# Splitting the 32x32 products of a triangular inverse over several steps, and copying accumulator banks out earlier, in a one-core decoder trunk

## The chip, the cores and the metric

The kernel runs on one core of a Trainium2 chip. The metric is the device time of one execution in microseconds (us), as the median of several runs.

The engines are named as the profile names them. PE is the matrix engine (PEld its weight loads), DVE the vector engine, ACT the scalar engine with its tables of functions, POOL the third elementwise engine, and SP the engine that here only issues DMAs. PSUM is the accumulator memory into which PE writes: eight banks, each of 128 partitions x 512 f32. SBUF is the on-chip memory for everything else.

## The reference, cut to what matters

One layer of a decoder trunk over 512 tokens of width 2048. The hidden state `h` goes through one wide projection, whose columns feed two token mixers. The change is almost wholly in the second, the chunked gated delta rule (GDN): per head and chunk it solves a unit lower triangular system, and its output is gated by `silu(z)`.

```python
p = h @ w_in[l]
c_q, c_kv, k_pe, q_g, k_g, v_g, z, b_logit, a_logit, gate_logits = _split_cols(p)
y_a = _mla_branch(c_q, c_kv, ...) @ w_o_mla[l]
y_b = _gdn_branch(qkv, z, ...) @ w_o_gdn[l]
...
# inside the GDN branch
Lmat = jnp.where(strict, jnp.einsum('bhncd,bhnsd->bhncs', kb, k) * decay, 0.0)
A = Lmat + jnp.eye(CHUNK, dtype=jnp.float32)
sol = lax.linalg.triangular_solve(A, rhs, left_side=True, lower=True, unit_diagonal=True)
...
o = o * lax.rsqrt(jnp.mean(o * o, axis=-1, keepdims=True) + EPS) * gdn_norm
o = o * jax.nn.silu(z)
...
# the channel mixer
gate, up = jnp.split(h @ w_gate_up[l], 2, axis=-1)
x = x + gt_f * ((jax.nn.silu(gate) * up) @ w_down[l])
```

## The kernel before, in words

**Products.** Every large product keeps about f32 accuracy by splitting each operand into a rounded high part and a remainder (`hi`, `lo`), and issuing three matmuls (hi x hi, hi x lo, lo x hi). Weights come in by DMA (`raw`), ACT casts `hi` (L270, or L1888 in the Strassen products), DVE subtracts to get `lo` (L271, L1895). A "set" of units accumulates over k in four PSUM banks and hands them to a `done` function.

**Order.** PE, POOL and SP instructions keep the order in which the program is written; ACT and DVE instructions are placed by the compiler's scheduler around them, which also assigns PSUM banks and SBUF slots. The order of PE is made by `Driver`. It runs the units of the big products one after the other; whenever 12 matmuls have been counted (`GROUP`), it calls `pump`, which gives each of the side chains (Python generators in the list `drv.chains`, in the order in which they were added) one step. `yield n` in a chain means that it sits out n steps. `hold` at the end of a set takes 12 off the count, so that the first step after it comes a group later. A chain's matmuls therefore stand between matmuls of the big product, in one lump per step.

**The GDN chain** (`gdn(g)`, once for heads 0 to 3 and once for heads 4 to 7). It makes `LT`, solves the 32x32 diagonal blocks on DVE (`fsX`, L801 to L808), writes the result to DRAM by two POOL DMAs (`fso`, L810) and reads it back by four POOL DMAs into the four 32-partition strips of `T32` (L814). Fourteen steps later 32 matmuls of 32x32 form `M1` in one PSUM bank (L823 to L830), ACT copies it out (L832, L833); six steps later 64 matmuls of 32x32 form `X1` in another bank (L835 to L844), from which ACT and DVE write into `T64` and `T64T`. The profile leaves numbers out of names, so `M1` stands there as `M`, `X1` as `X`, and `T32` as `T` (as does `T64`). An f32 matmul is counted as two instructions in the profile, so a lump of 32 shows as x64.

The first group's chain runs beside the sets `k47` and `v47` (profile names `k` and `v`), the second group's beside `cq`, `ckv` and `z1` (`cq`, `ckv`, `z`). Next to it in the second case run the chains that transpose the normed `cq` and `ckv` (`cT`, L986 to L993, one bank for each of four k, read by ACT at L249 and DVE at L250) and the rope chain, which puts two transposed tiles into two banks (`kpT`, L1046 to L1050).

**The z sets.** When set `z0` or `z1` ends, `z_done` applies silu to the four banks, straight from PSUM, on ACT (L946). The banks are free for the next sets only after that. After `z0` comes the set `cq`.

**The last transposed bank.** In the channel mixer, gate products are transposed in PSUM (`turned_a`, name `aT`). For blocks s < 8 a bank is copied to SBUF (`f`, L2165); for the others it is split straight from PSUM, by an ACT cast and a DVE subtraction (`hilo`, L244 and L247). The last such bank is s = 10, b = 3. After it begins the first Strassen down product, whose four products take all eight banks.

Of the kernel before, what the change touches and what calls it, by code (L numbers as in the profile page):

```python
# [11 lines left out]
AF = mybir.ActivationFunctionType  # L12
# [5 lines left out]
NT = 4  # L18
# [155 lines left out]
def block_kernel(ctx: ExitStack, tc: tile.TileContext, a: dict, out):  # L174
    nc = Core(tc, PINNED)
# [12 lines left out]
    def nm(s):  # L188
        serial[0] += 1
        return f"{s}_{serial[0]}"  # L190

    def S(s, dt=F32):
        return slots.tile([P, 512], dt, tag="s", name=nm(s))

    def PS(s):
        return psum.tile([P, 512], F32, tag="ps", name=nm(s))
# [7 lines left out]
    def side(dst, src):  # L204
        nc.gpsimd.dma_start(dst, src)

    def behind(ins):
        return tc.keep_in_program_order(ins)
# [3 lines left out]
    def tok(j):  # L212
        return slice(j * P, (j + 1) * P)
# [26 lines left out]
    def hilo(src, name, scale=None, late=False):  # L240
        hi, lo = S(name + "h", F32R), S(name + "l", F32R)
        n = src.shape[1]
        if scale is None:
            cast = nc.scalar.copy(hi[:, 0:n], src)  # L244
            if late:
                behind(cast)
            nc.vector.tensor_tensor(lo[:, 0:n], src, hi[:, 0:n].bitcast(F32), ALU.subtract)  # L247
        else:
            nc.scalar.activation(hi[:], src, AF.Copy, scale=scale)  # L249
            nc.vector.scalar_tensor_tensor(lo[:], src, scale, hi[:].bitcast(F32), op0=ALU.mult, op1=ALU.subtract)  # L250
        return hi, lo
# [454 lines left out]
    def gdn(g):  # L706
# [82 lines left out]
        for hf in range(2):  # L789
            s = S("fsL")  # L790
# [22 lines left out]
        for b in range(4):  # L813
            side(T32[32 * b:32 * b + 32, :].rearrange("p (n a) -> p n a", a=32),  # L814
                                fso[g][b].rearrange("c h i a -> i (c h) a"))
        yield 14
        T64 = [S("T64"), S("T64")]
        T64T = [S("T64T"), S("T64T")]
        for w in T64 + T64T:
# [2 lines left out]
        nc.vector.transpose(T32T[:], T32[:])  # L822
        p1 = PS("M1")  # L823
        for c in range(NT):
            for i in range(4):
                n0 = 128 * c + 32 * i
                for pa in (0, 64):
                    pb = pa + 32
                    mm(p1[pb:pb + 32, n0:n0 + 32], LT[c][pa:pa + 32, 128 * i + pb:128 * i + pb + 32],
                       T32[pa:pa + 32, n0:n0 + 32], start=True, stop=True, tile_position=(pa, pb))  # L830
        M1 = S("M1")
        nc.scalar.copy(M1[32:64, :], p1[32:64, :])  # L832
        nc.scalar.copy(M1[96:128, :], p1[96:128, :])  # L833
        yield 6
        p2 = PS("X1")  # L835
        for c in range(NT):
            for i in range(4):
                n0 = 128 * c + 32 * i
                s = slice(n0, n0 + 32)
                for pa in (0, 64):  # L840
                    pb = pa + 32
                    A_, B_ = slice(pa, pa + 32), slice(pb, pb + 32)
                    mm(p2[B_, s], T32T[B_, s], M1[B_, s], start=True, stop=True, tile_position=(pb, pb))
                    mm(p2[A_, s], M1[B_, s], T32T[B_, s], start=True, stop=True, tile_position=(pb, pa))  # L844
        v32 = lambda ap: ap.rearrange("p (n a) -> p n a", a=32)
        v64 = lambda ap: ap.rearrange("p (n a) -> p n a", a=64)
        for hf in range(2):
# [29 lines left out]
        for hf in range(2):  # L877
# [6 lines left out]
            for c in (2 * hf, 2 * hf + 1):  # L884
                nc.vector.tensor_scalar(h4(TT[c][:])[0:64, :, 64:128], v64(p4[0:64, 256 * (c % 2):256 * (c % 2) + 256]),
                                        -1.0, None, op0=ALU.mult)
        del T64, T64T, T32, T32T, M1, M2, LT
        yield
# [52 lines left out]
    def z_done(g, chain):  # L941
        def done(ps):
            sz = []
            for t in range(NT):
                s = S("sz")
                nc.scalar.activation(s[:], ps[t][:], AF.Silu)  # L946
                sz.append(s)

            def gen():
                while chain() in drv.chains:  # L950
                    yield
                for t in range(NT):
                    o = S("oz")
                    nc.scalar.dma_start(o[:], o_dram[t, g])
                    yield
                    for i in range(4):
                        nc.vector.scalar_tensor_tensor(sz[t][:, tok(i)], o[:, tok(i)], fo[:, t, 4 * g + i:4 * g + i + 1],
                                                       sz[t][:, tok(i)], op0=ALU.mult, op1=ALU.mult)
                    nc.scalar.dma_start(u_dram[t, g], sz[t][:])
                    yield  # L960
            drv.add(gen())
        return done
# [697 lines left out]
    def mixing():  # L1660
# [25 lines left out]
        def start_a():  # L1686
            ch["A"] = drv.add(gdn(0))
# [6 lines left out]
        def start_b():  # L1694
            ch["B"] = drv.add(gdn(1))
# [444 lines left out]
    def turned_a(b):  # L2140

        box = {}

        def one(n):
            if not turning:
                return
            s, tiles = turning[0]
            if s == 0:
                if b < 2:
                    gu_turn(1, b, tiles, n, box)  # L2150
                elif (b, n) == (3, 3):
                    turning.pop(0)
                return
            x, t = divmod(n, 2)
            if n == 0:
                box["ps"] = PS("aT")
            if s < 8:
                h, f = b % 2, 2 * (b // 2) + x
            else:
                h, f = x, b  # L2160
            nc.tensor.transpose(box["ps"][:, tok(n)], tiles[h, t][:, tok(f)], ident)
            if n == 3:
                if s < 8:
                    f_ = S("f")
                    nc.scalar.copy(f_[:], box["ps"][:])  # L2165
                    side(f_dram[2 * s + b // 2, h], f_[:])
                    stored.add((2 * s + b // 2, h))
                else:
                    kept_a(4 * s + b, hilo(box["ps"][:], "a"))
                if b == 3:  # L2170
                    turning.pop(0)

        return [lambda n=n: one(n) for n in range(4)]

    def kept_a(k, hl):

        if 36 <= k < 40:
            aT[k] = hl
        else:
            for i in range(2):  # L2180
                side(a_dram[k - 32, i], hl[i][:].bitcast(F32))
# [95 lines left out]
    def gu_turn(s, h, f, n, box):  # L2277

        x, t = divmod(n, 2)
        if n == 0:  # L2280
            box["ps"] = PS("guT")
        nc.tensor.transpose(box["ps"][:, tok(n)], f[h][:, 256 * t + 128 * x:256 * t + 128 * x + 128], ident)
        if n == 3:
            f_ = S("f")
            nc.scalar.copy(f_[:], box.pop("ps")[:])
            del f[h]
            side(f_dram[s, h], f_[:])
            stored.add((s, h))
# [334 lines left out]
```

## Time and profile before

| | |
|---|---|
| time, median of 3 runs | 2711.08 us (2708.78 to 2713.11) |
| the profiled execution | 2706.44 us, of which 2704.6 us from first to last instruction (the span) |
| granted PE clock | 0.999 of full |
| PE busy | 2683.6 us, 99% of the span, 13046 matmuls |
| PEld busy | 2237.3 us, 83% |
| DVE busy | 2087.6 us, 77% |
| ACT busy | 1201.6 us, 44% |
| POOL busy | 228.6 us, 8% |

In a line of the timeline, the first number is the start in us from the start of the span, the second the time taken, then the engine, the line of the kernel, the operation and "output <- inputs"; in brackets stands how long the engine sat idle before, and what ended that. All PE instructions pass through a helper and carry L157, so tile names tell them apart. A 128x512 matmul lasts about 0.39 us, but matmuls overlap: one starts every 0.227 us.

### The profile page before, as it was taken

The numbers are of one execution on the slowest core, as the hardware profiler recorded it, in microseconds if no ns is written. First come the engines' busy times: TensorE is split into PE (matmuls) and PEld (weight loads), VectorE is DVE, ScalarE is ACT, GpSimd is POOL, SyncE is SP. The second block draws the span as 40 slices with busy tenths as digits, with TensorE's granted clock in tenths as the row PEclk, the third lists the DMA queues.
The fourth block names the chain that finished last, engine by engine and source line by source line (L and its number), as shares of the span: only waits on it lengthen the run. The fifth ranks groups of instructions, "written<-read, shape, count | busy, mean of one in ns | idle before, by whom it ended". The sixth has DMA issues, their size and how long they took to land.

```text
span 2704.6 us, 36528 instructions
## 1 busy us (share of the span) xinstructions
PE 2683.6 (99%) x13046; PEld 2237.3 (83%) x13046; DVE 2087.6 (77%) x3230; ACT 1201.6 (44%) x1720; POOL 228.6 (8%) x310
## 2 busy tenths in 40 slices
PE   9999999999999999999999999999999999999998
PEld 7888788888888888888888888888888888888886
DVE  8785666777768866768788778788878888788786
ACT  3443432453245333234574444444444446545454
POOL 0000002011100000000010000001101101011012
PEclk9999999999999999999999999999999999999999
DMA  9897565646664867854763566567767777788595
GB/s 372 306 351 268 158 192 177 201 152 191 187 172 136 286 223 285 306 187 134 272 193 120 193 209 208 202 218 250 243 227 263 252 249 212 210 238 226 179 278 154
DMA packets 312126, 600.45 MB, mean 222 GB/s; under 512 B 42852, under 2 KB 69636, under 8 KB 311816
## 3 DMA queue, kind: packets, MB, share of 16 engines
q1 hardware_dynamic: 257160, 486.52, 54.7%
q0 software_dynamic: 21888, 59.83, 8.3%
q10 hardware_dynamic: 32896, 51.78, 5.2%
q8 instruction: 102, 1.67, 0.3%
q14 instruction: 80, 0.66, 0.1%
HBM read 507.80 MB, written 90.20 MB: 221 GB/s over the span
## 4 chain that ended last, share of the span: by engine, by line
PE 98%; DVE 1%; ACT 1%; issue 0%; DMA 0%; SPq 0%; DVEq 0%; ACTq 0%
PE m L157 43%; PE gb L157 6%; PE v L157 4%; PE z L157 3%; PE ya L157 3%; PE ga L157 3%; PE k L157 3%; PE s L157 3%; PE q L157 3%; PE yb L157 3%; PE wo L157 3%; PE gu L157 3%; PE dn L157 2%; PE qk L157 2%; PE dnt L157 2%; PE ckv L157 2%
## 5 line engine op out<-in xcount | busy, mean ns | idle before, releaser
L1888 ACT CAST hi<-raws 128x1024 fp32r<-128x1024 f32 (+1 forms) x360 | 322.9, 907 | 575.3 <-DVE raws L1868 346.9
L1895 DVE TENSOR_TENSOR lo<-raws,hi 128x1024 fp32r<-128x1024 f32 (+1 forms) x360 | 376.0, 1046 | 176.5 <-ACT hi L1888 168.9
L270 ACT CAST hi<-raw 128x1024 fp32r<-128x1024 f32 x262 | 271.9, 1041 | 489.8 <-DMA raw<-in_w_in_dram 130.7
L271 DVE TENSOR_TENSOR lo<-raw,hi 128x1024 fp32r<-128x1024 f32 x262 | 320.7, 1227 | 190.2 <-ACT hi L270 183.6
L442 DVE CUSTOM_DVE_ANT_0 rawm<-rawm,cbc 128x1024 f32<-128x1024 f32 x192 | 233.9, 1234 | 3.8 <-DMA rawm<-in_w_mod_dram 3.5
L157 PE MATMUL m<-hi,h2h 128*128 128x512 f32 x480 | 190.7, 397 | 0.0
L157 PE MATMUL m<-hi,h2l 128*128 128x512 f32 x480 | 187.4, 390 | 0.0
L157 PE MATMUL m<-lo,h2h 128*128 128x512 f32 x480 | 186.9, 389 | 0.0
L157 PE MATMUL m<-hi,xh 128*128 128x512 f32 x448 | 174.6, 390 | 0.7 <-DVE al L247 0.7
L157 PE MATMUL m<-hi,xl 128*128 128x512 f32 x448 | 174.4, 389 | 0.0
L157 PE MATMUL m<-lo,xh 128*128 128x512 f32 x448 | 174.4, 389 | 0.0
L1895 DVE TENSOR_TENSOR lo<-sums,hi 128x1024 fp32r<-128x1024 f32 x120 | 146.7, 1222 | 22.2 <-ACT hi L1888 22.1
L1868 DVE TENSOR_TENSOR sums<-raws,raws 128x1024 f32<-128x1024 f32 x120 | 146.2, 1219 | 3.6 <-DMA raws<-in_w_down_dram 3.6
L1888 ACT CAST hi<-sums 128x1024 fp32r<-128x1024 f32 x120 | 126.1, 1051 | 36.1 <-PE m L157 22.5
L157 PEld LDWEIGHTS m<-hi,h2l 128*128 128x128 f32 x480 | 90.1, 188 | 19.4
L157 PEld LDWEIGHTS m<-lo,h2h 128*128 128x128 f32 x480 | 90.4, 188 | 17.8
L157 PEld LDWEIGHTS m<-hi,h2h 128*128 128x128 f32 x480 | 90.2, 188 | 17.3
L157 PE MATMUL gb<-hh,hi 128*128 128x512 f32 x256 | 102.4, 400 | 0.0
L157 PE MATMUL gb<-hh,lo 128*128 128x512 f32 x256 | 100.0, 391 | 0.0
L157 PE MATMUL gb<-hl,hi 128*128 128x512 f32 x256 | 99.9, 390 | 0.0
L157 PEld LDWEIGHTS m<-hi,xh 128*128 128x128 f32 x448 | 84.1, 188 | 18.8 <-DVE al L247 1.1
L157 PEld LDWEIGHTS m<-hi,xl 128*128 128x128 f32 x448 | 84.1, 188 | 17.6
(587 smaller groups left out, 6844.5 us busy)
## 6 DMA issues: line engine op xcount, KB each, us to landing
raws<-in_w_gate_up_dram SPq DMA_DIRECT2D x400, 256.0 KB, 4.0
rawm<-in_w_mod_dram SPq DMA_DIRECT2D x192, 512.0 KB, 5.5
raw<-in_w_in_dram SPq DMA_DIRECT2D x144, 512.0 KB, 5.0
raws<-in_w_down_dram SPq DMA_DIRECT2D x160, 256.0 KB, 5.2
s_dram<-raws ACTq DMA_DIRECT2D x88, 256.0 KB, 3.5
raws<-s_dram SPq DMA_DIRECT2D x88, 256.0 KB, 4.3
rawa<-in_w_in_dram SPq DMA_DIRECT2D x32, 512.0 KB, 5.6
raw<-in_w_o_dram SPq DMA_DIRECT2D x24, 512.0 KB, 6.9
```

The source lines that it names most:

```text
L157: return self.tc.keep_in_program_order(f(*args, **kwargs))
L270: nc.scalar.copy(hi[:], raw[:])
L271: (lo_eng or nc.vector).tensor_tensor(lo[:], raw[:], hi[:].bitcast(F32), ALU.subtract)
L442: r = nc.vector.tensor_tensor_reduce(raw, raw, c, 1.0, 0.0, ALU.mult, ALU.add, parts[:, k, half:half + 1])
L1868: add = lambda o, x, y: behind(nc.vector.tensor_tensor(o, x, y, ALU.add))
L1888: nc.scalar.copy(hi[:], src)
L1895: nc.vector.tensor_tensor(lo[:], src, hi[:].bitcast(F32), ALU.subtract)
```

## The change

Three edits, in `gdn`, `z_done` and `turned_a`.

1. The four banks of `z0` are copied to SBUF, t = 0 and 2 by DVE and t = 1 and 3 by ACT. Silu is applied to the SBUF tiles in the first step of the z chain, which yields once more for that. `z1` is as it was.
2. The copy of the bank s = 10, b = 3 to SBUF is an ACT copy of its own, and the cast and the subtraction read that SBUF tile.
3. The `M1` products start two steps earlier and come in two parts in consecutive steps; the `X1` products come in four parts in four consecutive steps, the first 4 steps after the last `M1` part, where they were one lump 6 steps after. The last part of `X1` comes in the same step as the whole lump did before, and what follows keeps its steps.

```diff
@@ gdn
-        yield 14
+        yield 12
         T64 = [S("T64"), S("T64")]
...
                     mm(p1[pb:pb + 32, n0:n0 + 32], LT[c][pa:pa + 32, 128 * i + pb:128 * i + pb + 32],
                        T32[pa:pa + 32, n0:n0 + 32], start=True, stop=True, tile_position=(pa, pb))
+            if c == 1:
+                yield
         M1 = S("M1")
         nc.scalar.copy(M1[32:64, :], p1[32:64, :])
         nc.scalar.copy(M1[96:128, :], p1[96:128, :])
-        yield 6
+        yield 4
         p2 = PS("X1")
         for c in range(NT):
...
                     mm(p2[B_, s], T32T[B_, s], M1[B_, s], start=True, stop=True, tile_position=(pb, pb))
                     mm(p2[A_, s], M1[B_, s], T32T[B_, s], start=True, stop=True, tile_position=(pb, pa))
+            if c < NT - 1:
+                yield
@@ z_done
                 s = S("sz")
-                nc.scalar.activation(s[:], ps[t][:], AF.Silu)
+                if g:
+                    nc.scalar.activation(s[:], ps[t][:], AF.Silu)
+                else:
+                    (nc.scalar.copy if t % 2 else nc.vector.tensor_copy)(s[:], ps[t][:])
                 sz.append(s)
...
                 while chain() in drv.chains:
                     yield
+                if not g:
+                    for t in range(NT):
+                        nc.scalar.activation(sz[t][:], sz[t][:], AF.Silu)
+                    yield
                 for t in range(NT):
@@ turned_a
-                    kept_a(4 * s + b, hilo(box["ps"][:], "a"))
+                    src = box["ps"]
+                    if s == 10 and b == 3:
+                        src = S("f")
+                        nc.scalar.copy(src[:], box["ps"][:])
+                    kept_a(4 * s + b, hilo(src[:], "a"))
```

## The prediction

> **What bounds the kernel now.** I read the page first: the busy shares, then the chain that ended last. From them the question is only what PE does and waits for.
>
> ```profile
> PE 2683.6 (99%) x13046; PEld 2237.3 (83%) x13046; DVE 2087.6 (77%) x3230; ACT 1201.6 (44%) x1720; POOL 228.6 (8%) x310
> ...
> PE 98%; DVE 1%; ACT 1%; issue 0%; DMA 0%; SPq 0%; DVEq 0%; ACTq 0%
> ```
>
> PE is busy 2683.6 of 2704.6 us, so 21 us is all that waits could give back; the rest is matmuls, and the change removes none of those. Next I read whom PE waited for, in the list of waits of PE:
>
> ```profile
> PE cb L157 <- DMA crow<-in_c_dram: 3.0, 1, 3.0
> PE cT L157 <- DVE cql L250: 1.6, 1, 1.6
> ...
> PE cq L157 <- ACT sz L946: 0.9, 1, 0.9
> ...
> PE m L157 <- DVE al L247: 0.7, 1, 0.7
> ...
> PE cq L157 <- ACT E L766: 0.3, 1, 0.3
> ```
>
> Four of these rows lie where the change works: `cq` behind the silu of `z0`, `m` behind the last transposed bank, `cT` in the step that also holds the `X` lump, and `cq` behind `E`. They sum to 3.5 us. A measurement of this kernel can tell about 0.2%, or 5.4 us, from no change. So these waits cannot make a measurable gain even if all go; the question is what the new order of PE costs. I price each edit in PE time, because whatever PE loses is the kernel's time.
>
> **Edit 1, the z0 banks.** From the timeline around the end of `z0`:
>
> ```profile
> 636.85 0.40 PE L157 MATMUL cq<-hi,hl 128*128 128x512 f32 x1
> ...
> 636.94 0.60 ACT L766 ACTIVATE E<-pE 128x512 f32<-128x512 f32 x1
> 637.55 1.28 ACT L946 ACT_TABLE_LOAD   x1
> ...
> 637.59 0.50 PE L157 MATMUL cq<-hi,hh 128*128 128x512 f32 x1 [0.34 <-ACT E L766]
> ...
> 638.16 0.39 PE L157 MATMUL cq<-hi,hl 128*128 128x512 f32 x1
> ...
> 638.85 0.60 ACT L946 ACTIVATE sz<-z 128x512 f32<-128x512 f32 x1
> ...
> 639.49 0.50 PE L157 MATMUL cq<-hi,hh 128*128 128x512 f32 x1 [0.95 <-ACT sz L946]
> ...
> 639.83 0.39 PE L157 MATMUL cq<-lo,hh 128*128 128x512 f32 x1
> ```
>
> Matmuls normally start 0.227 us apart. From 638.16 to 639.49 is 1.33, so 1.10 us is lost, and the next distance of 0.34 loses 0.11 more: 1.2 us. The fourth bank of `cq` is the first of `z0`, and its silu comes only after the table load that ends at 638.83. With a copy on DVE there is no table load ahead of it. The DVE copy is program-later than the subtraction that DVE ends at about 636.9 (below, its idle time until `E`), and takes about 0.7 us (as `al` does below, also 128x512 from PSUM), so that bank is free at about 637.6, before PE asks for it. I take 1.2 us gained. The wait on `E` stays as it was, because `E` keeps its place; if the copies also change which bank `cq` gets, the loss there (637.59 against 636.85 + 0.23, and its slow restart, together 0.6) goes too, so 1.8 is the upper end. The lower end is nothing, if the copy is queued behind more.
>
> What is added costs nothing on PE: two ACT copies (1.2 us by the rows of 0.6), two DVE copies, four silus that move a step later, and the table load that moves with them. ACT is idle 2.39 us and DVE 0.68 us there:
>
> ```profile
> 637.57 1.13 DVE L776 SCALAR_TENSOR_TENSOR LT<-pkk,bp,E 128x128 f32<-128x128 f32 x4 [0.68 <-ACT E L766]
> ...
> 643.30 1.05 ACT L270 CAST hi<-raw 128x1024 fp32r<-128x1024 f32 x1 [2.39 <-PE cq L157]
> ```
>
> `LT` may begin 0.7 us later behind the copies; only its four DMA issues stand behind it. The extra step of the z chain delays the DRAM writes of `u`, which the trunk reads only after the attention. If this cover fails, a late `hi` cast costs PE at most the ACT copies, 1.2 us.
>
> **Edit 2, the last transposed bank.**
>
> ```profile
> 2293.39 0.59 ACT L244 CAST ah<-aT 128x512 fp32r<-128x512 f32 x1
> ...
> 2294.97 0.39 PE L157 MATMUL m<-hi,xl 128*128 128x512 f32 x1
> 2295.27 0.69 DVE L247 TENSOR_TENSOR al<-aT,ah 128x512 fp32r<-128x512 f32 x1
> 2295.39 1.05 ACT L1888 CAST hi<-raws 128x1024 fp32r<-128x1024 f32 x1 [1.41 <-DVE raws L1868]
> ...
> 2296.01 0.50 PE L157 MATMUL m<-hi,xh 128*128 128x512 f32 x1 [0.65 <-DVE al L247]
> ```
>
> From 2294.97 to 2296.01 is 1.04, so 0.81 is lost, and 0.11 for the restart: 0.9 us. The ACT copy takes the place of the cast at 2293.39, ends at 2293.98, and frees the bank a microsecond before PE wants it. The cast that follows takes another 0.59 of the 1.41 us in which ACT is idle, so the next `hi` is not late. Gain 0.9 us; lower end 0, if ACT puts the copy behind other work.
>
> **Edit 3a, more lumps.** Each lump pays to leave and re-enter the big product:
>
> ```profile
> 529.70 0.39 PE L157 MATMUL v<-hh,lo 128*128 128x512 f32 x1
> 530.01 0.21 PE L157 MATMUL X<-M,T32T 32*32 32x32 f32 x1
> ...
> 531.11 0.19 PE L157 MATMUL X<-T32T,M 32*32 32x32 f32 x1
> ...
> 531.23 0.50 PE L157 MATMUL v<-hh,hi 128*128 128x512 f32 x1
> 531.57 0.40 PE L157 MATMUL v<-hl,hi 128*128 128x512 f32 x1
> ```
>
> Entry costs 530.01 - 529.70 - 0.23 = 0.08, exit 0.12, restart 0.11: 0.31 us beyond the products' own 1.10 us, which stay the same in parts. There are four more parts in each group: one of `M`, three of `X`. In the second group the three `X` parts come just ahead of `cT` transposes, whose own restart is paid already (their rows are below), so 0.20 each. Sum 5 x 0.31 + 3 x 0.20 = 2.15 us lost. [...]
>
> [...]
>
> **Edit 3b, T32 is asked for earlier.** A step is 12 matmuls, 2.72 us, so the first `M` part moves 5.44 us earlier. In the first group `T32` has been there for long. In the second:
>
> ```profile
> 742.10 0.39 PE L157 MATMUL z<-hi,hh 128*128 128x512 f32 x1
> ...
> 747.63 1.20 PE L157 MATMUL M<-T,LT 32*32 32x32 f32 x64
> ```
> ```profile
> 732.91 1.06 POOL L157 DMA_DIRECT2D fso<-fsX  x1 [4.65 <-issue]
> 740.09 2.59 POOL L157 DMA_DIRECT2D T<-fso  x4 [6.13 <-DMA fso<-fsX]
> ```
> ```profile
> 746.58 0.71 DVE L822 STREAM_TRANSPOSE T32T<-T 128x512 f32<-128x512 f32 x1 [0.90 <-DMA T<-fso]
> ```
> ```profile
> DMA to landing us min/median/max: 2.4/2.4/4.4
> ```
>
> The old lump began 747.63, one microsecond after all of `T32` had landed. The 24th matmul before it starts at 742.10, so PE arrives at about 742.2. The four DMAs start 0.65 apart from 740.09; the first part reads strips 0 and 2, and the third DMA starts at 741.39 and lands 2.4 later, 743.8. PE then waits about 1.7 us. If it waits for the whole tile, it is until 746.58: 4.4 us. Lower end 0, if this DMA chain, which hangs on DVE's solve, is quicker. I take 1.7, because a read of a strip needs its strip alone. Behind the waiting `M` part on PE stands all of `z1`; everything that DVE and ACT prepare gets slack.
>
> **Edit 3c, a bank held three steps longer.** `X1` takes its bank with the first part, 3 steps earlier. In the second group banks are short: `z1` has four, and the two `kpT` banks, filled in the step of the old `M` lump, are read only at 804:
>
> ```profile
> L1049 ACT CAST kp<-kpT x2: 587/590/592, 804.1 to 804.6; 128x512 fp32r<-128x512 f32 x2
> ```
> ```profile
> 764.29 0.60 PE L157 MATMUL cT<-kc,cq 128*128 128x128 f32 x4
> 764.72 0.60 PE L157 MATMUL cT<-kc,ckv 128*128 128x128 f32 x4
> ...
> 769.22 0.66 PE L157 MATMUL cT<-kc,cq 128*128 128x128 f32 x4
> 771.44 0.66 PE L157 MATMUL cT<-kc,ckv 128*128 128x128 f32 x4 [1.56 <-DVE cql L250]
> ```
>
> Two banks are left, and at 769.22 `X` holds one: the two `cT` tiles of that step must share the last, and the second waits until ACT and DVE have read the first. It starts 2.22 after it instead of 0.43: 1.8 us lost. At 764.29 the same pair runs without a wait, since `X` has not begun. After the change `X` holds its bank there, so this pair waits as well: 1.8 us more. Ends 0 (another bank is free) to 2.7, which is the time from 764.72 to the end of the read of that `cq` tile by DVE at 767.4:
>
> ```profile
> L250 DVE SCALAR_TENSOR_TENSOR cql<-cT,columns,cqh x4: 735/748/751, 766.7 to 780.6; 128x512 fp32r<-128x512 f32 x4
> ```
>
> The `cT` of a step earlier could wait up to 1.6 on its predecessor's read; I put it at 0, as PE comes later by then.
>
> **Sum.** -1.2 - 0.9 + 2.15 + 1.7 + 1.8 = +3.5 us on the profiled execution's 2706.44, so 2710.0. That execution lies 4.6 below the median of the runs, 2711.08; by the median I forecast 2714.6, +0.13%, within what can be told from no change.
>
> **The rivals.**
> Slower: the first `M` part of the second group waits for all four strips of `T32`, 4.4 us instead of 1.7. The place is PE at 742.2; the sum becomes +6.2, with 2.7 for the bank +7.1, so 2717.3 to 2718.2. It decides once that wait passes 3.6 us, a landing after 745.8. For it speak the one slow landing of 4.4 us and the 6.13 us that POOL waited for `fso`, which a busier DMA can stretch; against it that the slow one is the fourth strip, which the first part does not read.
> Gains only: banks and `T32` are in time (the scheduler places banks anew, and DVE's solve shifts with PE), and only the lumps cost: -1.2 - 0.9 + 2.15, so 2711.1. For it speaks that the `cT` pair ran unhindered at 764.29; against it the two `kpT` banks.
> The first edit does nothing: the copies are placed behind `E` and `cq` waits on them as it did on silu. Then 3.5 + 1.2 = +4.7, 2715.8. Against it speaks DVE's idle time before 637.57.
> Last, the scheduler may order ACT and DVE anew all over. Since PE has 21 us of idle time in all, this can cost more than it gives.
>
> **How the numbers follow.** Forecast 0.42, the slower rival 0.26, gains only 0.18, first edit without effect 0.07, reordering 0.07. The forecast, gains only and the third rival are inside 5.4 us, save for a tenth where the ends meet; reordering is split evenly. A gain above 5.4 would need all the waits and more. That gives faster 0.07, same 0.62, slower 0.31. The range takes in -1.8 - 0.9 + 0 = -2.7 at one end, with runs 2 us either side of their median, and at the other 2.5 + 4.4 + 2.7 - 0.9, +8.7, with as much: 2706.5 to 2721.5.
>
> **What would show it.** In the profile after: no rows `cq` behind `sz` and `m` behind `al` (edits 1 and 2 right); `M` lumps of x32 and `X` parts of a quarter each, each 0.2 to 0.3 us beyond its products; a new wait of PE at `M` behind the DMA of `T` of 1.7 us, in the second group only; the wait of `cT` behind `cql` twice. I am wrong if `M` starts at once, if `cT` waits no more than before, or if new waits stand at weights (`hi`, `lo`) elsewhere.

## Result and profile after

| | before | after |
|---|---|---|
| time, median of 21 runs each | 2710.20 us (2707.77 to 2714.29) | 2713.84 us (2712.54 to 2719.59) |
| ratio of the times | 1 | 1.0016, 95% interval 1.0009 to 1.0023 |
| the profiled execution | 2706.44 us, span 2704.6 us | 2715.18 us, span 2713.4 us |
| granted PE clock | 0.999 | 0.998 |

The change costs 0.16%, 4.3 us (2.4 to 6.2), where +3.5 was forecast. The ratio goes by the means of the runs; the two medians are 3.6 us apart. The interval leaves out 1, so a change of this size can be told from none, which the prediction did not think possible below 0.2%. The two profiles are 8.7 us apart, which is more than the change: before's profiled execution was 3.8 us below its median, after's 1.3 above. To see where it arises I set the start of each PE matmul in one trace against the start of the same matmul in the other. Of the difference 2.1 us is there by 18 us, in the first product, 490 us ahead of the first edit. Some 1.6 of it is PE at half its clock, in this window of after (start and end; length; busy time and count of PE, PEld, DVE, ACT, POOL; granted clock; DMA share; GB/s):

```profile
14.20:17.70 3.50, 3.50 (x10) 2.75 (x9) 3.01 (x8) 1.67 (x2) 0.00 (x0) 0.51 1.04 418
```

The same is in four of the other traces below, with and without the third edit, and not in the rest (before has 1.00 in this window), so it goes with the execution. About 1.5 us come in small steps between 1100 and 2620, far from the edits, which come and go from kernel to kernel. The rest is where the edits are: -1.8 at the end of `z0`, -0.9 at the last transposed bank, +1.3 at the parts of the first group, +2.1 at `M` and +4.5 at `X` and `cT` in the second: together +5.2.

From the page of after, the busy time of the engines and the chain that ended last:

```profile
PE 2690.7 (99%) x13046; PEld 2239.6 (83%) x13046; DVE 2087.8 (77%) x3232; ACT 1203.3 (44%) x1723; POOL 234.6 (9%) x310
...
PE 92%; DVE 3%; DMA 2%; issue 1%; ACT 1%; SPq 0%; ACTq 0%; POOL 0%; DVEq 0%; POOLq 0%
```

PE has the same 13046 matmuls as before and is busy 7.1 us longer, while its idle time (span less busy) grew only from 21.0 to 22.7. So most of the loss does not stand in a list of waits: matmuls and the ways between them took longer, some of them at half the clock. The list of PE's waits in after (total, times, longest, in us):

```profile
PE cT L157 <- DVE cql L250: 3.7, 2, 2.1
PE cb L157 <- DMA crow<-in_c_dram: 3.0, 1, 3.0
PE M L157 <- DMA T<-fso: 1.4, 2, 0.9
```

The rows of `cq` behind `sz`, `cq` behind `E` and `m` behind `al` are gone, `M` behind the DMA of `T` is new, and `cT` behind `cql` is there twice. The timeline of after at the end of `z0`:

```profile
635.90 0.69 DVE L953 COPY sz<-z 128x512 f32<-128x512 f32 x1
...
639.09 1.28 ACT L766 ACT_TABLE_LOAD   x1
...
640.30 0.39 PE L157 MATMUL cq<-hi,hl 128*128 128x512 f32 x1
...
640.38 0.60 ACT L766 ACTIVATE E<-pE 128x512 f32<-128x512 f32 x1
640.53 0.40 PE L157 MATMUL cq<-hi,hh 128*128 128x512 f32 x1
...
641.97 1.28 ACT L961 ACT_TABLE_LOAD   x1
...
643.26 0.64 ACT L961 ACTIVATE sz<-sz 128x512 f32<-128x512 f32 x1
```

DVE copies the first bank four microseconds before `E`, and the `cq` matmuls run on 0.23 apart while ACT still loads tables and makes `E`. The last transposed bank:

```profile
2302.10 0.59 ACT L2183 COPY f<-aT 128x512 f32<-128x512 f32 x1
...
2303.68 0.39 PE L157 MATMUL m<-hi,xl 128*128 128x512 f32 x1
...
2303.91 0.39 PE L157 MATMUL m<-hi,xh 128*128 128x512 f32 x1
2303.98 0.69 DVE L247 TENSOR_TENSOR al<-f,ah 128x512 fp32r<-128x512 f32 x1
```

The bank is free at 2302.69, and `m` no longer waits for `al`. The `M` parts of the second group:

```profile
741.76 2.59 POOL L157 DMA_DIRECT2D T<-fso  x4 [4.57 <-DMA fso<-fsX]
...
743.50 0.39 PE L157 MATMUL z<-hi,hl 128*128 128x512 f32 x1
...
744.36 0.21 PE L157 MATMUL M<-T,LT 32*32 32x32 f32 x2 [0.47 <-DMA T<-fso]
...
745.51 0.69 PE L157 MATMUL M<-T,LT 32*32 32x32 f32 x30 [0.94 <-DMA T<-fso]
...
746.13 0.50 PE L157 MATMUL z<-hi,hh 128*128 128x512 f32 x1
```

PE waits twice, and the part is done by 746.13. The four DMAs of `T`, one for each strip, start 0.65 apart and land 2.4 us later (the DMA view of `T` in after, 735 to 752):

```profile
DMA to landing us min/median/max: 2.4/2.4/2.5
```

So the strips are there at about 744.2, 744.8, 745.5 and 746.1, and PE starts at 744.36 and 745.51, with the first and the third. PE waited for the two strips that the part reads, one after the other, and not for the tile. The steps that hold `X` and `cT`:

```profile
765.80 0.66 PE L157 MATMUL cT<-kc,ckv 128*128 128x128 f32 x4
...
766.21 0.48 PE L157 MATMUL z<-hi,hh 128*128 128x512 f32 x1
...
767.67 0.39 PE L157 MATMUL z<-hi,hh 128*128 128x512 f32 x1
...
769.50 0.66 PE L157 MATMUL cT<-kc,cq 128*128 128x128 f32 x4
...
770.35 1.23 DVE L271 TENSOR_TENSOR lo<-raw,hi 128x1024 fp32r<-128x1024 f32 x1 [2.38 <-ACT hi L270]
...
771.49 0.75 DVE L250 SCALAR_TENSOR_TENSOR cql<-cT,columns,cqh 128x512 fp32r<-128x512 f32 x1
...
772.29 1.11 PE L157 MATMUL cT<-kc,ckv 128*128 128x128 f32 x4 [2.13 <-DVE cql L250]
...
773.06 0.78 PE L157 MATMUL z<-hi,hh 128*128 128x512 f32 x1
...
775.61 0.40 PE L157 MATMUL z<-hi,hh 128*128 128x512 f32 x1
```

The second `cT` tile of the pair waits until DVE has read the first, 2.36 us longer than the undisturbed 0.43. DVE is late because a `lo` subtraction of 1.23 us stands ahead of the read. Behind the wait PE is slow: four transposes take 0.77 (772.29 to 773.06) where they take 0.41 at 765.80, and six `z` matmuls 2.55 where they take 1.46 from 766.21. That is 1.45 us more. Windows of after there:

```profile
768.00:772.00 4.00, 2.16 (x42) 1.41 (x40) 1.65 (x2) 1.63 (x2) 0.56 (x2) 1.00 0.35 101
772.00:773.60 1.60, 1.31 (x5) 1.25 (x6) 1.37 (x3) 0.16 (x1) 0.00 (x0) 0.50 0.45 105
773.60:775.60 2.00, 2.00 (x6) 1.55 (x5) 1.44 (x2) 0.53 (x1) 0.00 (x0) 0.55 0.73 257
775.60:778.00 2.40, 2.40 (x43) 1.71 (x41) 0.45 (x2) 0.32 (x1) 0.00 (x0) 1.00 0.81 231
```

The granted clock is 0.50 for some 3.4 us, and then full again. A mean of 0.998 over the span does not show it.

### The profile page after: what moved, and what is told of

It reads as the page before. It is cut to its first block, busy times and chain, and to the rows that moved or that the text cites. A ratio compares the mean times of both kernels' runs of the same rounds, so it can differ in the third digit from the quotient of the medians.

```text
span 2713.4 us, 36539 instructions
## 1 busy us (share of the span) xinstructions
PE 2690.7 (99%) x13046; PEld 2239.6 (83%) x13046; DVE 2087.8 (77%) x3232; ACT 1203.3 (44%) x1723; POOL 234.6 (9%) x310
## 4 chain that ended last, share of the span: by engine, by line
PE 92%; DVE 3%; DMA 2%; issue 1%; ACT 1%; SPq 0%; ACTq 0%; POOL 0%; DVEq 0%; POOLq 0%
PE m L157 41%; PE gb L157 6%; PE v L157 4%; PE s L157 3%; PE k L157 3%; PE ya L157 3%; PE ga L157 3%; PE q L157 3%; PE yb L157 3%; PE wo L157 3%; PE z L157 3%; PE gu L157 3%; PE dn L157 2%; PE qk L157 2%; PE dnt L157 2%
## 5 line engine op out<-in xcount | busy, mean ns | idle before, releaser
L157 PEld LDWEIGHTS m<-lo,xh 128*128 128x128 f32 x448 | 84.1, 188 | 18.6 <-DVE lo L1906 1.3
```

Of the source, the lines that this page charges most:

```text
L157: return self.tc.keep_in_program_order(f(*args, **kwargs))
```

## The experiments

My theory: the edits at `z0` and at the last bank gain their waits (1.8 and 0.9 us), and the parts cost three things of their own: ways in and out of the big product, the early wait for `T32`, and a bank that `X` holds too long while `kpT` holds two. The rival is that the scheduler's new order of ACT and DVE makes the difference, so that undoing one part would not give its cost back. All ratios are to runs of before on the same chip. "Gain" and "loss" at a place are from the starts of the same matmuls in two profiled executions.

**The edits at z0 and the last bank alone.** Against after, it puts the products back:

```diff
-        yield 12
+        yield 14
...
-            if c == 1:
-                yield
...
-        yield 4
+        yield 6
...
-            if c < NT - 1:
-                yield
```

> The z0 copies and the copied last bank, without the parts (M and X lumps as before). Theory 1, PE pays at the places of the edit: from the two traces, PE gains 1.8 us at the start of cq and 0.8 us at the last bank, so 2.6 us below before (ratio 0.9990), with no wait of cq on sz or E and none of m on al, and the wait of cT on cql once, 1.6 us, as before. Theory 2, the scheduler's new order of ACT and DVE sets the difference: new waits of PE of a microsecond or more at weights after 1300 us, and a ratio anywhere between 0.999 and 1.002.

Measured: 2709.16 us (11 runs), ratio 0.9994 (0.9986 to 1.0003): no change that can be told. `z0` gained 1.8 us and the last bank 0.9, as in after, but PE's waits have two new entries:

```profile
PE cT L157 <- DVE ckvl L250: 1.8, 2, 1.1
PE cT L157 <- DVE cql L250: 1.6, 1, 1.6
...
PE gb L157 <- DVE yl L247: 0.7, 1, 0.7
```

At 765 the `cT` tiles, which ran freely before, wait for the reads of earlier ones and lose 2.2 us. So in this execution the gain at `z0` was lost again 125 us later, where banks are short. That the edits bring this about is not shown: ACT reads the first `ckv` tile 5.2 us after it was begun (2.9 in before), behind a `hi` cast that waits for its weights to land, and in two executions of one kernel below the same distance is 3.6 and 7.4. The times can't decide it, since the interval holds the 0.9990 that was expected.

**The parts alone.** Before with the third edit only (the diff above, reversed).

> The parts of M and X alone; z0 and the last bank as before. Theory 1: PE loses 1.3 us in the first group, 2.1 us at M in the second and 4.5 us from the first X part to the last cT transpose there, so 7.9 us above before (ratio 1.003); the waits of PE are M behind the DMA of T (about 1.4 us) and cT behind cql twice (3.7 us). Theory 2: 2 to 6 us, and the losses lie elsewhere as well. On either, e1 and e2 together should make the change: -2.6 + 7.9 = 5.3 us.

Measured: 2716.57 us (9 runs), ratio 1.0025 (1.0016 to 1.0035). The loss is the parts': 1.3 us in the first group, 1.5 at `M`, 6.3 at `X` and `cT`. PE waits for `cql` 3.7 us in two, and for `T` 0.8. Here the clock fell behind both waits, also behind the one of 1.56 us (windows of this kernel):

```profile
775.60:778.00 2.40, 2.40 (x7) 1.63 (x5) 0.90 (x2) 0.00 (x0) 0.00 (x0) 0.52 0.85 236
...
780.00:782.00 2.00, 1.28 (x7) 1.08 (x8) 1.46 (x3) 1.10 (x3) 0.00 (x0) 0.83 0.09 37
782.00:784.00 2.00, 2.00 (x6) 1.62 (x5) 1.22 (x3) 0.62 (x2) 0.00 (x0) 0.50 0.00 0
```

The ratios of these two, 0.9994 and 1.0025, multiply to 1.0019, the whole change's 1.0016 within its interval.

**M in parts, X in one lump; and the reverse.**

`M` in parts, against before:

```diff
-        yield 14
+        yield 12
...
+            if c == 1:
+                yield
...
-        yield 6
+        yield 7
```

> The kernel before with the M products alone in two parts, two steps and one step earlier; X in one lump in its old step. Theory 1 (parts and waits priced one by one): 0.3 us in the first group, and in the second 0.3 us and a wait of M for T of 0.8 to 1.7 us, so 1.5 to 2.3 us from the first M part to the kpT transposes; cT waits on cql once, 1.6 us, as before. Rival (the early M part also sets off the longer cT wait): cT waits twice.

`X` in parts, against before:

```diff
-        yield 6
+        yield 3
...
+            if c < NT - 1:
+                yield
```

> The kernel before with the X products alone in four parts; M in one lump in its old step. Theory 1: no wait at M; 0.9 us in the first group; in the second 0.6 us for the parts, a second wait of cT on cql of 1.8 to 2.1 us, and 1 to 2 us at half clock behind it: 3.5 to 4.7 us there. Rival as in e3: cT waits once, and only the 1.5 us of the parts are lost.

Measured, one execution each, with 2711.28 for before beside them: 2711.79 with `M` in parts, 2717.32 with `X` in parts. `M` in parts lost 0.3 us in the first group and 1.3 in the second, with a wait for `T` of 0.7, a little under what was expected; `cT` waits once, 1.6, as before, though in this execution the clock fell behind it, to 0.50 from 776 to 778, and cost 1.6 more. `X` in parts lost 1.0 in the first group (0.33 a part) and 4.7 in the second, with no wait for `T` and two waits of `cT`. So the second `cT` wait belongs to `X`, and the wait for `T` to `M`.

**The first M part one step later.** Against after:

```diff
-        yield 12
+        yield 13
...
-        yield 4
+        yield 3
```

> The changed kernel with the first M part one step later (the parts in the steps 13 and 14, X where the change has it). Theory 1: PE reaches the first M part 2.7 us later, and the longest wait for T seen was 1.4 us, so it goes; PE is 1.4 to 2 us ahead of the changed kernel at the kpT transposes. The two cT waits stay, perhaps longer, since PE comes to them earlier. Rival: the wait moves along, because PE's pace sets when T lands.

Measured: 2710.77 us in one execution (before 2711.28). The wait for `T` is gone, and the `M` parts lose 0.33 us instead of 2.1. `X` and `cT` lose 4.7, about as in after (4.5).

**kpT 17 steps later, in four combinations.** The two `kpT` banks are filled and then sit unread until ACT copies them to SBUF, into the tile `kp`. The pool of `kp` (`wide`) has one slot, and `cbc` lives there too. The timeline of after shows what the copy waits for:

```profile
811.14 1.22 DVE L442 CUSTOM_DVE_ANT_0 rawm<-rawm,cbc 128x1024 f32<-128x1024 f32 x1
...
812.40 1.07 ACT L1060 CAST kp<-kpT 128x512 fp32r<-128x512 f32 x2 [2.77 <-DVE parts L442]
```

It starts when DVE ends the last pass over `cbc` (`parts` is the result of that pass); in before the same pass ends right ahead of it, at 804.1. Filled from 752.57, the banks are held for 60 us. This edit puts the same transposes and copies into a chain of their own that sits out 17 steps:

```diff
-        kp = wides.tile([P, 4, 512], F32R, tag="wide", name="kp")
-        for j, part in enumerate(kr):
...
+        def kp_gen():
+            yield 17
+            kp = wides.tile([P, 4, 512], F32R, tag="wide", name="kp")
+            for j in range(2):
...
+        drv.add(kp_gen())
```

With the whole change:

> The changed kernel, but the kpT transposes in a chain of their own 17 steps later, so that their two banks are free while the cT chains run. Theory 1, the cT transposes wait because X holds one of the two banks left: both waits of cT on cql go (3.7 us of idle PE), and with them the about 1 us of half clock behind the longer one, so 4.7 us below the changed kernel, about 1 us below before. Rival, the wait is DVE's queue (the sums of the modulation columns stand ahead of the cT subtractions): PE still waits for cql, 1 to 2 us each time, and the time is that of the changed kernel, 4 us above before.

Without the parts:

> e1 with the kpT transposes 17 steps later. Theory 1 (banks): the one wait of cT on cql that the kernel before has goes too, 1.8 us with its restart, so 2.6 + 1.8 = 4.4 us below before (ratio 0.9984). Rival (DVE's queue): the wait stays, the time is that of e1. If the two banks are missed where the transposes now stand, there is a new wait of qpe, v or att there, and part of this is lost.

With the whole change and the first `M` part one step later; without the parts, once more; and on before alone:

> The whole change, with the first M part one step later (its wait for T gone) and the two kpT tiles transposed 17 steps later in a chain of their own (the cT waits gone). If the parts cost only their way in and out of the big product, this lies 5 x 0.31 + 3 x 0.20 = 2.2 us above the kernel of edits 1 and 2 with kpT later (ratio 0.9984), so at 0.9992 of before, with no rows cT behind cql and M behind T. If the split of M and X costs more than its parts and its two waits, it is at 0.9999 or above, as the whole change with kpT later was. If the parts cost nothing once the waits are gone, it equals the kernel without them, 0.9984.

> Edits 1 and 2 with the kpT tiles 17 steps later, once more, beside the two others of this call. If its 0.9984 is the kernel's own, it comes out between 0.9975 and 0.9992 again, and below both others. If it was that chip's order, it lies at 0.9995 or above.

> The kernel before with nothing but the kpT tiles 17 steps later. If the two banks that kpT holds are what the rest waits on, the cT wait of 1.6 us goes and the gains add up: this gains about 1.6 (0.9994), and edits 1 and 2 add 1.8 + 0.9 us, to 0.9984. If edits 1 and 2 give nothing of their own (as without the kpT edit, 0.9994 with an interval that holds 1), this is at 0.9984 too.

| kernel | median | ratio to before |
|---|---|---|
| whole change | 2713.84 us | 1.0016 (1.0009 to 1.0023) |
| whole change, kpT later | 2706.47 us | 0.9990 (0.9981 to 0.9999) |
| whole change, kpT later, M a step later | 2707.46 us | 0.9991 (0.9982 to 1.0000) |
| z0 and last bank, kpT as before | 2709.16 us | 0.9994 (0.9986 to 1.0003) |
| z0 and last bank, kpT later | 2705.82 us | 0.9984 (0.9975 to 0.9992) |
| the same again | 2706.31 us | 0.9985 (0.9976 to 0.9994) |
| before with kpT later | 2707.43 us | 0.9995 (0.9986 to 1.0004) |

With `kpT` later the whole change goes from 1.0016 to 0.9990, and in its trace PE has no wait at `cT`. That is 7 us (about 4 to 10), more than the 4.7 expected, which the interval holds. The rival was that DVE's queue makes the wait, and its trace decides between them. The pair that waited longest in after, here:

```profile
766.45 0.66 PE L157 MATMUL cT<-kc,cq 128*128 128x128 f32 x4
...
766.95 0.60 PE L157 MATMUL cT<-kc,ckv 128*128 128x128 f32 x4
...
768.45 0.74 DVE L250 SCALAR_TENSOR_TENSOR cql<-cT,columns,cqh 128x512 fp32r<-128x512 f32 x1
```

DVE reads the first tile as late as in after (2.74 us from its start to the end of the read, in both), but the second tile starts 0.50 after the first and does not wait for the read. So what the second tile waits for in after is a free bank, and the late read only sets how long. The kernel of edits 1 and 2 with `kpT` later is faster than both kernels of this study, twice. The expectation for the `M` part a step later came out in the middle (0.9992 forecast, 0.9991 measured), but its interval overlaps both of its neighbours, so the cost of the parts alone, about 2 us, is read from the traces and not shown by the times; taking the wait for `T` away as well gave nothing that the times can tell. Nor do the times alone tell edits 1 and 2 (0.9985) from none (0.9995).

One caution comes from the kernel that was run twice: its two profiled executions have spans of 2700.7 and 2705.3 us, and PE's waits of the second hold rows that the first lacks:

```profile
PE gb L157 <- DVE yl L247: 1.4, 1, 1.4
...
PE hss L157 <- DVE sq L1353: 1.0, 1, 1.0
PE cT L157 <- DVE cql L250: 1.0, 1, 1.0
```

So waits of a microsecond come and go between executions of one program, and the rival has that much truth: a single profile can't tell such a wait from an edit. Behind two of them PE also ran at half its clock, which it did not there in the first execution, and with that they make some 4.1 of the 4.6 us between the two:

```profile
903.30:906.80 3.50, 3.30 (x8) 2.62 (x9) 3.50 (x10) 1.53 (x2) 0.00 (x0) 0.51 1.04 396
...
1364.10:1367.60 3.50, 3.50 (x18) 3.50 (x19) 2.83 (x12) 0.21 (x1) 0.01 (x1) 0.51 0.21 53
```

What held in every kernel with `X` in parts and `kpT` as before is two `cT` waits, the longer of 2.1.

**A longer wait, nothing else.** Before with one read of a `cT` bank issued twice on DVE, so that its successor waits longer:

```diff
                     res.append(hilo(p[:], "c" + which, norm[:, k:k + 1]))
+                    if which == "q" and k == 1:
+                        h_, l_ = res[-1]
+                        nc.vector.scalar_tensor_tensor(l_[:], p[:], norm[:, k:k + 1], h_[:].bitcast(F32), ...)
```

> The kernel before, with the subtraction of one cq tile issued twice on DVE (the same values are written again), so that the one cT wait on cql is longer by a DVE pass of 0.7 us: 2.2 to 2.3 us instead of 1.6. Theory: a wait of about 2.1 us or more of PE brings the half clock that stands behind the longer wait in the changed kernel, so granted clock 0.5 for 2 to 4 us behind it, and 1 to 2 us more lost than the wait itself. Rival: the half clock comes from what goes before (the small X products), and a longer wait alone leaves the clock at 1.0.

Measured: 2710.28 us in one execution (before 2711.28). The wait of PE and the windows around it:

```profile
PE cT L157 <- DVE cql L995: 2.9, 1, 2.9
```
```profile
770.00:772.00 2.00, 0.00 (x0) 0.00 (x0) 1.94 (x6) 1.10 (x3) 0.00 (x0) 1.00 0.78 216
772.00:774.00 2.00, 1.31 (x5) 1.25 (x6) 1.28 (x3) 0.73 (x3) 0.00 (x0) 0.53 0.72 245
774.00:776.00 2.00, 2.00 (x7) 1.63 (x6) 0.75 (x1) 0.50 (x1) 0.00 (x0) 0.61 0.18 72
776.00:778.00 2.00, 2.00 (x13) 1.65 (x12) 0.00 (x0) 0.51 (x1) 0.00 (x0) 1.00 0.00 0
```

With no part of the change in the kernel, the clock fell behind a wait of 2.9 us, to 0.53 from 772 to 774. The wait grew by 1.33 and the place lost 2.66, so the half clock cost 1.3 us. The total time did not show it: 2.7 us is inside what one execution varies. It is one execution, and in `M` in parts the clock fell behind before's own wait, 1.60 there.

## Why the prediction was right, step by step

| step | forecast | trace of after | what the runs say |
|---|---|---|---|
| edit 1, z0 banks | -1.2 (to -1.8) | -1.8 | gains the same without the parts |
| edit 2, last bank | -0.9 | -0.9 | the same without the parts |
| 3a, ways in and out | +2.15 | +2.3 | 0.33 a part in `X` of the first group |
| 3b, wait for T32 | +1.7 | +1.7 | gone with `M` a step later |
| 3c, bank held longer | +1.8 (to 2.7) | +2.36, and 1.45 of half clock | gone with `kpT` later |
| sum | +3.5 | +5.2 | +4.3 (2.4 to 6.2) by the times |

The sign and each mechanism held, and the times allow the sum; two terms were mis-sized. That the median came out within 1 us of the 2714.6 forecast is partly luck: the errors of the two terms, -0.6 and +2.0, partly cancel, and the forecast stands on a median of three runs that lies 0.9 above that of 21.

*Edit 1* took its upper end. The prediction kept the wait on `E`, saying that it goes only if `cq` gets another bank; the row is gone, and `cq` runs on while `E` is made. Which bank `cq` got is not in the trace.

*Edit 3a.* The first group lost 1.3 for four parts, 0.33 each against 0.31; the `M` part of the second group 0.33 (with the wait taken away). The three `X` parts ahead of `cT` moved the offset by 0.5 each, of which 0.275 are their products (a quarter of 1.10): 0.22 each against the 0.20 that I took. In all 1.3 + 0.33 + 0.67. That is between the forecast's 2.15 and the 2.5 of the range, which is 0.31 for all eight parts. The exit from `X` into `cT` took 0.12 us in after (765.68 to 765.80), as much as the exit into the big product, but a part ahead of transposes did not pay the restart a second time, 0.22 against 0.33. The range's other end, 0 for the parts, is shown by no run: where no wait stood beside them, in `X` of the first group, they cost 0.33 each.

*Edit 3b.* From the last `z` matmul at 743.50 to the next at 746.13 are 2.63 us; with the part a step later the same stretch is 0.94. The wait thus costs 1.7, though the list of waits has only 1.4, because it counts idle time between matmuls' ends. PE waited strip by strip: the slower rival, which let it wait for all four strips, is ruled out by the start at 745.51, with the third landing. Had it been so, this execution would have lost only some 0.6 more, since here the fourth strip landed as fast as the others.

*Edit 3c* is the term that failed in size. I reckoned the new wait like the old one, 2.22 between the two tiles instead of 0.43. It was 2.79, since DVE had a `lo` subtraction ahead of the read; and I did not foresee that PE would run at half its clock (0.50) behind the wait. Together 3.8 us for 1.8.

"Gains only" fell with the two new waits. That the first edit does nothing is refuted too at its place, though in the one trace without the parts and with `kpT` as before its 1.8 us were lost again at the `cT` tiles.

## What to carry to other kernels

On an engine that is 99% busy, a wait removed can be lost again at the next scarce thing downstream: here, in the trace of the first two edits alone, the gain at one bank was gone again at the next shortage of banks, and with the two banks freed that sat unread for 55 to 60 us the loss of the whole change turned into a gain of 0.1%. So look for the tile that holds the scarce resource longest without being read, before making anything finer; by tile, the profile shows when it was filled and when it was read. Splitting a lump of small matmuls cost about 0.3 us a part here, 0.2 ahead of transposes, and it spread the second group's `X` products over 15.65 us in after (761.71 to 777.36), where the lump's in before stood within 1.10 (768.00 to 769.10).

## What the hardware did that I had not expected

PE's granted clock fell to about 0.50 behind a wait of 2.1 us (in after, the parts alone, `X` in parts, and the whole change with `M` a step later) or 2.9 us (the longer wait), for some 3.4 us, and that cost 1.3 to 1.7 us in addition to the wait. After a wait of 1.6 us it fell in two executions (`M` in parts, 1.60, and the second wait of the parts alone, 1.56) and stayed at 1.00 in others: before, the edits at `z0` and the last bank alone, and the second wait of after, of `X` in parts and of the whole change with `M` a step later. In the kernel that was run twice it fell to 0.51 even behind the 1.4 at `gb` and the 1.0 at `hss`, and in the first product of after behind two gaps of 0.94 and 0.79. The window of before, behind its wait of 1.56 us that ended at 771.44:

```profile
772.00:774.00 2.00, 2.00 (x11) 1.64 (x11) 1.39 (x3) 1.31 (x3) 0.00 (x0) 1.00 0.76 232
```

In the first product of before the two gaps were 1.21 and 0.80, and the clock stayed at 1.00 behind them. So the length of the wait alone does not decide whether the clock falls, and what else does is not shown.

The falls also go with the spread of the times. Of the 31 runs of before beside the first experiments, 5 have a mean granted clock of 0.999 and take 2707.5 us on average, 21 have 0.998 and take 2710.1, and 5 have 0.997 and take 2712.2.
